# A two-layer streaming trunk on one core: operands turned by one full-height vector instruction per column block, then carried across partitions by 16 on-chip transfers begun by GpSimd

## The chip, the cores and the metric

The kernel runs on one core of one Trainium2 chip. The metric is the device time of an execution in microseconds; the number given for a kernel is the median of its runs. The core has TensorE (PE, with its weight loads PEld), VectorE (DVE), ScalarE (ACT), GpSimd (POOL) and SyncE (SP), which run their own instruction streams and meet at semaphores, and 16 DMA engines that move what the queues of SP, ACT or GpSimd are told to move.

## The reference, cut to what matters

256 tokens of width 2048 go through two layers; every layer adds a mixer, a SwiGLU feed-forward and a gated embedding to the running sum, all with an RMSNorm ahead. Everything is float32.

```
h = x                                        # (1, 256, 2048)
for i in range(2):
    h = h + mixer_i(rmsnorm(h))              # i = 0: top-k attention and gated linear attention
                                             # i = 1: stick-breaking attention, 16 heads of 128
    n = rmsnorm(h);  h = h + (silu(n @ W_gate) * (n @ W_up)) @ W_down        # 5632 wide
    h = h + (p[i] @ W_pe) * sigmoid(rmsnorm(h) @ W_pg)
out = rmsnorm(h)
```

## The kernel before, in words

The sum `h` lies in SBUF with the tokens on the partitions (two halves of 128 tokens, 2048 columns). A product `n @ W` wants the contraction on the partitions, so each stage's operand is `h` turned: 16 chunks of 128 columns, each [128 columns x 256 tokens], times the norm's gain, split in two parts that PE takes in one pass each (`aH` and `aL`). A weight is split likewise into `whi` and `wlo`, and every product is done as three matmuls: hi by hi (L201), hi by lo (L202) and lo by hi (L203).

The weights stream through `unit` (L176): SP loads 1 MB into `raw` (a ring of two), ACT casts it by halves into `whi` (L99), DVE subtracts into `wlo` (L100), rings of four. A half unit is two chunks by 512 output columns: 12 matmuls. A `block` is one block of 512 output columns over the whole contraction, 8 half units where it is 2048 deep.

All other work is filled in between. `later` puts a function into a queue and `tick`, at the end of each half unit, takes one from it; `delay` and `after` say how many half units must pass first; `need` takes what a product can't do without.

What is turned, and how:

- **h, for the norms n1 to n5.** When a column block of h is complete, `finish_cols` (L224) queues two calls of `turn_h` (L135): four PE transposes into PSUM (L141), then ACT writes `aH` (L146) and DVE `aL` (L147) per chunk. n1 leads from the first mixer into the FFN, n2 from the FFN into the embedding, n3 from there into the odd mixer, n4 and n5 as n1 and n2 in the second layer. The first norm, n0, does the same while x arrives.
- **The FFN's hidden blocks.** A block of 512 hidden columns is `sl` (ACT silu, times the up product on DVE, L802). `turn_blocks` (L123) turns it into `hx` by 16 DVE transposes of 32x256 (L128): DVE turns blocks of 32 by 32 and writes them into any quarter of the partitions. `split_hid` (L787) makes `hH` and `hL` of it. There are 11 blocks in each of two layers, in groups of 3, 3, 3 and 2; a group's down product comes a group later.
- **The odd mixer's q and k.** `tok` (L762) is the block scaled by the norm; 16 transposes of the same kind write `qT` or `kT`, 4 blocks each, which the scores on PE read.

`rstd_of` (L113) makes a norm's factor: two DVE instructions, then a power on GpSimd (L119). `ple` (L847) is the embedding; its first four blocks have a contraction of two chunks only, loads of 512 KB. In the last one `keep` (L892) holds the last 256 columns' weights in SBUF, loaded through a buffer of their own.

Of the kernel before, what the change touches and what calls it, by code (L numbers as in the profile page):

```python
# [27 lines left out]
def trunk_kernel(ctx: ExitStack, tc: tile.TileContext, x, p, even_norm, even_w_in, even_w_gk,  # L28
# [36 lines left out]
    # the activation tables and the tensor engine's clock are up when the data comes  # L65
# [7 lines left out]
    # norm gains, one row of 128 per chunk, turned so that a chunk's gains lie along the partitions  # L73
# [49 lines left out]
    def turn_blocks(dst, src, a):  # L123
# [3 lines left out]
        for q in range(4):  # L127
            nc.vector.transpose(dst[32 * a:32 * a + 32, :, :, 32 * q:32 * q + 32],  # L128
                                src.rearrange("p t (m a c) -> p t m a c", a=4, c=32)[32 * q:32 * q + 32, :, :, a, :])
# [5 lines left out]
    def turn_h(dst, norm, c2):  # L135
        """Chunks 2*c2 and 2*c2+1 of h, transposed, times the gain, split."""
# [39 lines left out]
    def unit(ps, stat, k0, cols, first, last, nk=KU, kw0=None, step=KU, pre=None):  # L176
        """nk chunks of the contraction: cols = [(weight, first column, width)]."""
# [28 lines left out]
    def block(stat, cols, nk=KC, key=None, ps=None, k0=0, k1=None, kw=0, pre=None):  # L206
        """Output columns over chunks k0..k1 of the contraction; returns the two PSUM tiles."""
# [43 lines left out]
    with tc.issue_after(got_gains.ins):  # L251
# [4 lines left out]
    # upb[s, c] = 1/16 where s <= c in one chunk of 64; sub[s, c] = 1/16 where s > c there  # L256
    upb = const.tile([P, P], F32, name="upb")
    nc.gpsimd.memset(upb, 0.0625)
    nc.gpsimd.affine_select(upb, upb, pattern=[[1, P]], compare_op=OP.is_ge, fill=0.0, base=0,
                            channel_multiplier=-1)  # L260
    nc.gpsimd.memset(upb[0:64, 64:128], 0.0)
    sub = stage("sub")[:, :P]
    nc.gpsimd.memset(sub, 0.0625)
    nc.gpsimd.affine_select(sub, sub, pattern=[[-1, P]], compare_op=OP.is_gt, fill=0.0, base=0,
                            channel_multiplier=1)
    nc.gpsimd.memset(sub[64:128, 0:64], 0.0)
    subr = const.tile([P, P], F32R, name="subr")
    nc.vector.tensor_copy(subr, sub)
    # keys no later than the query, in one chunk
    upm = upb.bitcast(I32)  # L270
    # strictly earlier keys, keys along the partitions
# [8 lines left out]
    # -1 where the first index is no earlier than the second  # L280
# [10 lines left out]
    def even_mixer(xs, ps0, ep):  # L291
# [3 lines left out]
        oT = new_act()  # L295

# [12 lines left out]
        def tokens(ps, name, w=NB):  # L309
            """The block's last w columns by tokens, scaled by the row's norm."""  # L310
# [672 lines left out]
```

## Time and profile before

| | |
|---|---|
| median of 3 runs | 2442.11 us (2441.62 to 2442.64) |
| span of the profiled execution | 2438.5 us |
| PE busy | 2417.6 us (99%) |
| DVE busy | 1506.6 us (62%) |
| ACT busy | 1154.1 us (47%) |
| GpSimd busy | 19.2 us (1%) |
| share of PE in the chain that ended last | 91% |
| 16 DMA engines, SP's queue | 55.6% |

The span is one execution, taken by the profiler; the median is of other executions, and 3.6 us longer. The chain is the work that ended last, followed back from the end: an engine that has no share in it may be late by something without a change of the time.

### The profile page before, as it was taken

To read this page: it belongs to the slowest core of one execution; us is meant where nothing else is said; L and a number is where in the kernel's file an instruction comes from. 1 tells how busy PE (TensorE), PEld (TensorE's weight loads), DVE (VectorE), ACT (ScalarE), POOL (GpSimd) and SP (SyncE) were. 2 spreads that over 40 slices of the span, in tenths; PEclk is the share of its full clock that TensorE was granted. 3 is DMA by queue.
4 is the path that set the end of the run, shared out by engine and by line. 5 is a ranking of instruction groups with operands and counts; after the bars stand their busy time and mean duration, and the time that the engine had idled before them with its cause. 6 is when DMAs were issued, how large, how long until landed. Compare 5 with 4: busy or idle time off the path is not lost.

```text
span 2438.5 us, 27647 instructions
## 1 busy us (share of the span) xinstructions
PE 2417.6 (99%) x10966; PEld 1996.5 (82%) x10966; DVE 1506.6 (62%) x1907; ACT 1154.1 (47%) x1418; POOL 19.2 (1%) x45
## 2 busy tenths in 40 slices
PE   8999999999999999999999999999999999999998
PEld 7887788888888888888888888888888888888887
DVE  5765555766756665655676666557667556556564
ACT  6644444344434434446546565544444344444463
POOL 0000000000000000000000000000000000000000
PEclk9999999999999999999999999999999999999999
DMA  6454455566556565555554454555655655556563
GB/s 211 147 169 151 144 194 186 189 196 201 189 192 193 186 205 183 198 190 185 178 190 156 161 184 165 180 190 177 203 190 192 205 190 186 196 187 206 182 231 123
DMA packets 231651, 450.01 MB, mean 185 GB/s; under 512 B 9457, under 2 KB 16337, under 8 KB 231394
## 3 DMA queue, kind: packets, MB, share of 16 engines
q1 hardware_dynamic: 231234, 447.07, 55.6%
q8 instruction: 86, 1.41, 0.2%
q10 hardware_dynamic: 288, 1.18, 0.1%
q14 instruction: 43, 0.35, 0.0%
HBM read 446.12 MB, written 2.10 MB: 184 GB/s over the span
## 4 chain that ended last, share of the span: by engine, by line
PE 91%; issue 5%; ACT 2%; DVE 1%; DMA 1%; SPq 0%; POOLq 0%; POOL 0%; DVEq 0%; ACTq 0%
PE mm L202 29%; PE mm L201 29%; PE mm L203 29%; PE at L141 1%; DVE kT L128 1%; DVE wlo L100 0%; DMA raw<-in_odd_w_in_dram 0%; PE at L424 0%; DMA h<-in_x_dram 0%; PE at L742 0%; DVE sp L719 0%; ACT whi L99 0%; ACT sp L716 0%; ACT sp L715 0%; ACT L715 0%
## 5 line engine op out<-in xcount | busy, mean ns | idle before, releaser
L100 DVE TENSOR_TENSOR wlo<-raw,whi 128x1024 fp32r<-128x1024 f32 (+2 forms) x848 | 1020.7, 1213 | 794.1 <-ACT whi L99 790.1
L99 ACT CAST whi<-raw 128x1024 fp32r<-128x1024 f32 (+2 forms) x848 | 874.8, 1042 | 1053.5 <-PE mm L203 668.8
L201 PE MATMUL mm<-whi,aH 128*128 128x512 f32 (+2 forms) x2656 | 1036.9, 390 | 0.7 <-ACT whi L99 0.7
L202 PE MATMUL mm<-wlo,aH 128*128 128x512 f32 (+2 forms) x2656 | 1028.8, 387 | 4.1 <-DVE wlo L100 4.1
L203 PE MATMUL mm<-whi,aL 128*128 128x512 f32 (+2 forms) x2656 | 1028.7, 387 | 0.0
L202 PEld LDWEIGHTS mm<-wlo,aH 128*128 128x128 f32 x2656 | 499.4, 188 | 104.7 <-DVE wlo L100 5.9
L203 PEld LDWEIGHTS mm<-whi,aL 128*128 128x128 f32 x2656 | 499.1, 188 | 103.4 <-issue 1.0
L201 PEld LDWEIGHTS mm<-whi,aH 128*128 128x128 f32 x2656 | 499.2, 188 | 102.9 <-issue 2.8
L201 PE MATMUL mm<-whi,hH 128*128 128x512 f32 x704 | 277.2, 394 | 0.0
L202 PE MATMUL mm<-wlo,hH 128*128 128x512 f32 x704 | 277.0, 393 | 0.0
L203 PE MATMUL mm<-whi,hL 128*128 128x512 f32 x704 | 273.6, 389 | 0.0
L128 DVE STREAM_TRANSPOSE hx<-sl 32x256 f32<-32x256 f32 x352 | 153.6, 436 | 6.1
L201 PEld LDWEIGHTS mm<-whi,hH 128*128 128x128 f32 x704 | 132.2, 188 | 30.0
L203 PEld LDWEIGHTS mm<-whi,hL 128*128 128x128 f32 x704 | 132.2, 188 | 29.7
L202 PEld LDWEIGHTS mm<-wlo,hH 128*128 128x128 f32 x704 | 132.4, 188 | 26.1
L146 ACT ACTIVATE aH<-at,gT 128x256 fp32r<-128x256 f32 x96 | 45.1, 473 | 51.4 <-DVE aL L147 47.5
L789 ACT CAST hH<-hx 128x1024 fp32r<-128x1024 f32 x22 | 23.2, 1054 | 92.6 <-DVE hx L128 92.6
L147 DVE SCALAR_TENSOR_TENSOR aL<-at,gT,aH 128x256 fp32r<-128x256 f32 x96 | 45.8, 480 | 22.0 <-ACT aH L146 21.9
L234 DVE TENSOR_TENSOR h<-mm,h 128x512 f32<-128x512 f32 x80 | 52.4, 682 | 2.7 <-PE mm L203 2.7
L141 PE MATMUL at<-ident,h 128*128 128x128 f32 x192 | 30.5, 283 | 5.0 <-DMA h<-in_x_dram 5.0
L141 PEld LDWEIGHTS at<-ident,h 128*128 128x128 f32 x192 | 24.9, 145 | 11.8 <-DMA h<-in_x_dram 3.0
L128 DVE STREAM_TRANSPOSE qT<-tok 32x256 f32<-32x256 f32 x64 | 27.9, 436 | 6.8 <-ACT tok L762 5.8
(221 smaller groups left out, 806.8 us busy)
## 6 DMA issues: line engine op xcount, KB each, us to landing
raw<-in_ffn_w_gate_dram SPq DMA_DIRECT2D x88, 1024.0 KB, 5.2
raw<-in_ffn_w_up_dram SPq DMA_DIRECT2D x88, 1024.0 KB, 5.2
raw<-in_ffn_w_down_dram SPq DMA_DIRECT2D x88, 1024.0 KB, 5.0
raw<-in_odd_w_in_dram SPq DMA_DIRECT2D x48, 1024.0 KB, 5.2
raw<-in_even_w_in_dram SPq DMA_DIRECT2D x36, 1024.0 KB, 5.0
raw<-in_ple_w_gate_dram SPq DMA_DIRECT2D x28, 1024.0 KB, 5.1
raw<-in_even_w_out_dram SPq DMA_DIRECT2D x16, 1024.0 KB, 5.1
raw<-in_odd_w_out_dram SPq DMA_DIRECT2D x16, 1024.0 KB, 5.0
```

The lines of the kernel that those rows point to most:

```text
L99: nc.scalar.copy(hi, raw)
L100: nc.vector.tensor_tensor(lo, raw, hi.bitcast(F32), OP.subtract)
L128: nc.vector.transpose(dst[32 * a:32 * a + 32, :, :, 32 * q:32 * q + 32], src.rearrange("p t (m a c) -> p t m a c", a=4, c=32)[32 * q:32 * ...
L141: nc.tensor.transpose(ps[:, c, tt, :], h[:, tt, k * P:(k + 1) * P], ident)
L146: nc.scalar.activation(dst[0][:, k, :], src, AF.Copy, scale=g)
L147: nc.vector.scalar_tensor_tensor(dst[1][:, k, :], src, g, dst[0][:, k, :].bitcast(F32), op0=OP.mult, op1=OP.subtract)
L201: nc.tensor.matmul(ps[tt][:, :n], sh, hi[:, c, :n], start=st, stop=False)
L202: nc.tensor.matmul(ps[tt][:, :n], sh, lo[:, c, :n], start=False, stop=False)
L203: nc.tensor.matmul(ps[tt][:, :n], sl, hi[:, c, :n], start=False, stop=en)
L234: nc.vector.tensor_tensor(hs, ps[tt], hs, OP.add)
L789: nc.scalar.copy(d[0], t)
```

## The change

`turn_h` stays for n0 alone. For n1 to n5, for the FFN's blocks and for q and k there is `cross`: one DVE transpose over all 128 partitions and 1024 elements of a block (L130) into `tq`, a single buffer, which turns each 32x32 block in its own 32 partitions; then 16 DMAs from SBUF to SBUF (L135), each of 32 partitions by 1 KB, begun by GpSimd, that carry the quarters of `tq` to the partitions where they belong, in `tx`, a ring of two. There are 20 crossings of h, 22 of hidden blocks and 8 of q and k: 50, with 800 DMAs. What reads the result comes two half units later at the earliest: `gain_h` (ACT L171, DVE L172) for h, `split_hid` (ACT L819, DVE L820), and for q and k one ACT copy (L794) into `qT` or `kT`, whose layout is now by heads.

To find room in SBUF, some things move: constants of the first mixer into its own pool, the scratch of the squares into a shared buffer, `gated` writes in place, and `keep` loads through the stream's `raw` ring. `mixer_out` is cut in two, so that the pool of `tq` and `tx` opens behind the first mixer.

```
+    def cross(src):
+        tq = pools["x"].tile([P, 4, NT, 4, 32], F32, name="tq", bufs=1)
+        nc.vector.transpose(tq.rearrange("p a t m r -> p t m a r"),
+                            src.rearrange("p t (m a c) -> p t m a c", a=4, c=32))
+        x = pools["x"].tile([P, 8, 4, 32], F32, name="tx")
+        for a in range(4):
+            for q in range(4):
+                nc.gpsimd.dma_start(x[32 * a:32 * a + 32, q::4], tq[32 * q:32 * q + 32, a])
+        return x
...
+    def gain_h(dst, norm, x, c2):
+        for k in (2 * c2, 2 * c2 + 1):
+            g = gT[1][:, (norm - 1) * KC + k:(norm - 1) * KC + k + 1]
+            src = crossed(x)[:, k % 4]
+            hi, lo = (flat(d[:, k:k + 1, :])[:, 0] for d in dst)
+            nc.scalar.activation(hi, src, AF.Copy, scale=g)
+            nc.vector.scalar_tensor_tensor(lo, src, g, hi.bitcast(F32), op0=OP.mult, op1=OP.subtract)
...
     def finish_cols(nx, cb):
+        x = {}
+        first = (nx["key"], "x", cb)
+        later(lambda: x.update(x=cross(h[:, :, cb * NB:(cb + 1) * NB])), key=first)
         for c2 in (2 * cb, 2 * cb + 1):
-            later(lambda c2=c2: turn_h(nx["dst"], nx["norm"], c2), key=(nx["key"], c2))
+            later(lambda c2=c2: gain_h(nx["dst"], nx["norm"], x["x"], c2), key=(nx["key"], c2), after=(first, 2))
...
-                for a in range(4):
-                    later(lambda t=t, d=dst, a=a: turn_blocks(d.rearrange("p t (m c) -> p t m c", c=P), t, a))
+                x = {}
+                later(lambda t=t, x=x: x.update(x=cross(t)), key=("x3", g, i))
+                later(lambda d=dst, x=x: nc.scalar.copy(flat(d), crossed(x["x"])), after=(("x3", g, i), 2))
...
-                hx = fp.tile([P, 4, NT * P], F32, name="hx")
-                for a in range(4):
-                    later(lambda d=hx, t=sl, a=a: turn_blocks(d.rearrange("p m (t c) -> p t m c", t=NT), t, a))
-                later(lambda t=hx, n=n, gi=gi: split_hid(hT[gi], t, 4 * n), key=("hT", i, b))
+                x = {}
+                later(lambda t=sl, x=x: x.update(x=cross(t)), key=("xT", i, b))
+                later(lambda x=x, n=n, gi=gi: split_hid(hT[gi], x["x"], 4 * n), key=("hT", i, b),
+                      after=(("xT", i, b), 2))
...
-            sgm = pp.tile([P, NB], F32, name="sgm", bufs=2)[:, :w]
-            nc.scalar.activation(sgm, pg[:, :w], AF.Sigmoid, scale=rs[:, tt:tt + 1])
-            nc.vector.tensor_tensor(sgm, sgm, eb[c0 // NB][tt][:, c0 % NB:c0 % NB + w], OP.mult)
+            nc.scalar.activation(pg[:, :w], pg[:, :w], AF.Sigmoid, scale=rs[:, tt:tt + 1])
+            e = eb[c0 // NB][tt][:, c0 % NB:c0 % NB + w]
+            nc.vector.tensor_tensor(e, pg[:, :w], e, OP.mult)
...
-            raw = pp.tile([P, KU, HB], F32, name="kept", bufs=1)
+            raw = wp.tile([P, KU, NB], F32, name="raw", bufs=2)[:, :, :HB]
```

How the instructions stand on the engines, at three places. First DVE at the first hidden block of the first FFN. Before (`sl` is the block, `hx` it turned, `wlo` the weights' low parts):

```order
L802 SCALAR_TENSOR_TENSOR sl_3289<-mm_3292,rstd_3287,sl_3289 128x512
L802 SCALAR_TENSOR_TENSOR sl_3289<-mm_3293,rstd_3287,sl_3289 128x512
L128 STREAM_TRANSPOSE hx_3432<-sl_3289 32x2x4x32 x8
L100 TENSOR_TENSOR wlo_3496<-raw_3473,whi_3495 128x1024
L128 STREAM_TRANSPOSE hx_3432<-sl_3289 32x2x4x32 x4
L100 TENSOR_TENSOR wlo_3518<-raw_3515,whi_3517 128x1024
L128 STREAM_TRANSPOSE hx_3432<-sl_3289 32x2x4x32 x4
L100 TENSOR_TENSOR wlo_3538<-raw_3515,whi_3537 128x1024
L790 TENSOR_TENSOR hL_3127<-hx_3432,hH_3126 128x1024
```

And now:

```order
L832 SCALAR_TENSOR_TENSOR sl_3328<-mm_3332,rstd_3326,sl_3328 128x512
L130 STREAM_TRANSPOSE tq_3507<-sl_3328 128x8x4x32
L100 TENSOR_TENSOR wlo_3545<-raw_3526,whi_3544 128x1024
L100 TENSOR_TENSOR wlo_3565<-raw_3562,whi_3564 128x1024
L100 TENSOR_TENSOR wlo_3581<-raw_3562,whi_3580 128x1024
L100 TENSOR_TENSOR wlo_3599<-raw_3596,whi_3598 128x1024
L100 TENSOR_TENSOR wlo_3615<-raw_3596,whi_3614 128x1024
L820 TENSOR_TENSOR hL_3157<-tx_3509,hH_3156 128x1024
```

The 16 transposes have become one, and what reads the turned block stands behind five half units' subtractions in place of three; on ACT the cast into `hH` stands behind the same five casts.

The second place is DVE at the end of the first FFN (n2), from the second column block of the down product to the third; `h_73` is h, `at` the PSUM tile of the PE transposes. Before:

```order
L100 TENSOR_TENSOR wlo_8044<-raw_8041,whi_8043 128x1024
L147 SCALAR_TENSOR_TENSOR aL_7730<-at_7965,gT5_95,aH_7729 128x256
L234 TENSOR_TENSOR h_73<-mm_7902,h_73 128x512
L147 SCALAR_TENSOR_TENSOR aL_7730<-at_7965,gT5_95,aH_7729 128x256
L234 TENSOR_TENSOR h_73<-mm_7903,h_73 128x512
L100 TENSOR_TENSOR wlo_8069<-raw_8041,whi_8068 128x1024
```

And now:

```order
L261 TENSOR_TENSOR h_73<-mm_7968,h_73 128x512
L261 TENSOR_TENSOR h_73<-mm_7969,h_73 128x512
L100 TENSOR_TENSOR wlo_8149<-raw_8130,whi_8148 128x1024
L130 STREAM_TRANSPOSE tq_8111<-h_73 128x8x4x32
L172 SCALAR_TENSOR_TENSOR aL_7791<-tx_8010,gT5_95,aH_7790 128x256 x4
L100 TENSOR_TENSOR wlo_8185<-raw_8182,whi_8184 128x1024
L100 TENSOR_TENSOR wlo_8213<-raw_8210,whi_8212 128x1024
```

Every column block's turn into `tq` now stands ahead of the reading of the block before it, and the weights' subtractions stand behind both.

The third place is GpSimd around n3, the norm between the embedding and the odd mixer. Before, from the end of the first mixer on:

```order
L667 TENSOR_TENSOR sg_2464<-sg_2464,gn_1703 128x512 x2
L119 TENSOR_TENSOR rstd_3287<-var_3284,mhalf_96 128x2
L119 TENSOR_TENSOR rstd_8351<-var_8348,mhalf_96 128x2
L119 TENSOR_TENSOR rstd_9046<-var_9043,mhalf_96 128x2
L119 TENSOR_TENSOR rstd_11858<-var_11855,mhalf_96 128x2
```

And now (`x16` is the 16 DMAs of one crossing; `rstd_9171` is n3's):

```order
L135 DMA tx_8849<-tq_8847 32x2x128 x16
L135 DMA tx_9032<-tq_9030 32x2x128 x16
L119 TENSOR_TENSOR rstd_9171<-var_9168,mhalf_96 128x2
L135 DMA tx_9217<-tq_9215 32x2x128 x16
L135 DMA tx_9379<-tq_9377 32x2x128 x16
```

The power for a norm now stands behind the 16 DMAs of the norm's last column block.

## Rows read from the trace of the kernel before

**Rows 1.** The page: engines' busy time, and the chain's shares by engine.
```profile
PE 2417.6 (99%) x10966; PEld 1996.5 (82%) x10966; DVE 1506.6 (62%) x1907; ACT 1154.1 (47%) x1418; POOL 19.2 (1%) x45
...
PE 91%; issue 5%; ACT 2%; DVE 1%; DMA 1%; SPq 0%; POOLq 0%; POOL 0%; DVEq 0%; ACTq 0%
```

**Rows 2.** Costliest groups: line, engine, operation, count | busy us, mean ns | idle before.
```profile
L128 DVE STREAM_TRANSPOSE hx<-sl 32x256 f32<-32x256 f32 x352 | 153.6, 436 | 6.1
...
L146 ACT ACTIVATE aH<-at,gT 128x256 fp32r<-128x256 f32 x96 | 45.1, 473 | 51.4 <-DVE aL L147 47.5
...
L141 PE MATMUL at<-ident,h 128*128 128x128 f32 x192 | 30.5, 283 | 5.0 <-DMA h<-in_x_dram 5.0
```

**Rows 3.** Timeline of PE around a group of transposes: start us, length us, what.
```profile
1085.65 0.40 PE L203 MATMUL mm<-whi,hL 128*128 128x512 f32 x1
1085.89 0.60 PE L141 MATMUL at<-ident,h 128*128 128x128 f32 x4
...
1086.80 0.39 PE L203 MATMUL mm<-whi,hL 128*128 128x512 f32 x1
```

**Rows 4.** Timeline of DVE at the first hidden block.
```profile
431.81 1.22 DVE L100 TENSOR_TENSOR wlo<-raw,whi 128x1024 fp32r<-128x1024 f32 x1 [1.50 <-ACT whi L99]
432.95 1.40 DVE L802 SCALAR_TENSOR_TENSOR sl<-mm,rstd,sl 128x512 f32<-128x512 f32 x2
```

**Rows 5.** Timeline of ACT at the first hidden block.
```profile
430.72 1.05 ACT L99 CAST whi<-raw 128x1024 fp32r<-128x1024 f32 x1 [1.67 <-PE mm L203]
433.44 1.05 ACT L99 CAST whi<-raw 128x1024 fp32r<-128x1024 f32 x1 [1.67 <-PE mm L203]
```

**Rows 6.** Timeline, DVE then ACT, at n1's last column block.
```profile
388.51 1.28 DVE L234 TENSOR_TENSOR h<-mm,h 128x512 f32<-128x512 f32 x2
...
388.96 1.06 ACT L99 CAST whi<-raw 128x1024 fp32r<-128x1024 f32 x1 [1.62 <-PE mm L203]
```

**Rows 7.** Timeline of DVE, two column blocks of n2.
```profile
1065.88 1.28 DVE L234 TENSOR_TENSOR h<-mm,h 128x512 f32<-128x512 f32 x2
...
1076.86 1.28 DVE L234 TENSOR_TENSOR h<-mm,h 128x512 f32<-128x512 f32 x2
```

**Rows 8.** Timeline, ACT then DVE, at n3's last column block.
```profile
1214.27 1.37 ACT L864 ACTIVATE sgm<-mm,rstd 128x512 f32<-128x512 f32 x2 [0.94 <-PE mm L203]
...
1216.28 1.29 DVE L867 TENSOR_TENSOR h<-h,sgm 128x512 f32<-128x512 f32 x2
...
1219.88 0.17 DVE L758 TENSOR_SCALAR rq<-rstd 128x2 f32<-128x2 f32 x1 [0.90 <-POOL rstd L119]
```

**Rows 9.** Timeline of ACT, the first group's k in the odd mixer.
```profile
1259.30 1.31 ACT L762 ACTIVATE tok<-mm,rstd 128x512 f32<-128x512 f32 x2 [0.54 <-PE mm L203]
```

**Rows 10.** Groups of GpSimd: line, operation, shape, count | busy us, mean ns | idle before.
```profile
L667 POOL TENSOR_TENSOR sg<-sg,gn 128x512 f32<-128x512 f32 x4 | 5.1, 1294 | 5.9 <-ACT sg L665 5.9
L119 POOL TENSOR_TENSOR rstd<-var,mhalf 128x2 f32<-128x2 f32 x6 | 4.2, 700 | 2052.0 <-DVE var L117 1327.7 <-ACT pe L856 724.3
L632 POOL TENSOR_TENSOR rso<-rso,mhalf 128x4 f32<-128x4 f32 x2 | 2.0, 1016 | 180.1 <-DVE rso L631 180.1
```

**Rows 11.** The chain at the start: start us, length us, what (SPq issues a load).
```profile
1.71 0.46 SPq L184
```

**Rows 12.** DMA queues (packets, MB, share); loads: count, KB each, median us to landing.
```profile
q1 hardware_dynamic: 231234, 447.07, 55.6%
...
raw<-in_ple_w_gate_dram SPq DMA_DIRECT2D x28, 1024.0 KB, 5.1
...
raw<-in_ple_w_proj_dram SPq DMA_DIRECT2D x8, 512.0 KB, 3.7
...
out_dram<-h SPq DMA_DIRECT2D x8, 256.0 KB, 2.8
...
graw<-in_odd_norm_dram SPq DMA_DIRECT2D x1, 8.0 KB, 1.6
```

More of the change, by code (lines that the diff above doesn't have):

```diff
@@ L107, in square_sum @@
             ss[key] = sm.tile([P, NT, 4], F32, name="ss")
-        scr = sm.tile([P, NB], F32, name="sqs", bufs=1)
+        scr = sm.tile([P, NB], F32, name="sqs", tag="stage", bufs=1)
         nc.scalar.activation(scr, src, AF.Square, accum_out=ss[key][:, tt, cb:cb + 1])
@@ L121, in rstd_of, with crossed, flat @@
         return rstds[key]
[L123 to L129, printed above, removed]
+    pools = {}
+    def cross(src):
[7 more added lines that the diff above has]
+        return x
+    def crossed(x):
+        return x.rearrange("p q m r -> p m q r")
+    def flat(t):
+        return t.rearrange("p m (q r) -> p m q r", q=8)
     def new_act():
@@ L253, in trunk_kernel @@
     done.update((("n0", i), 0) for i in range(KC // 2))
[L257 to L270, printed above, removed]
     diag = const.tile([P, P], F32, name="diag")
@@ L295, in even_mixer @@
         oT = new_act()
+        upb = ep.tile([P, P], F32, name="upb", bufs=1)
+        nc.gpsimd.memset(upb, 0.0625)
+        nc.gpsimd.affine_select(upb, upb, pattern=[[1, P]], compare_op=OP.is_ge, fill=0.0, base=0,
+                                channel_multiplier=-1)
+        nc.gpsimd.memset(upb[0:64, 64:128], 0.0)
+        sub = stage("sub")[:, :P]
+        nc.gpsimd.memset(sub, 0.0625)
+        nc.gpsimd.affine_select(sub, sub, pattern=[[-1, P]], compare_op=OP.is_gt, fill=0.0, base=0,
+                                channel_multiplier=1)
+        nc.gpsimd.memset(sub[64:128, 0:64], 0.0)
+        subr = ep.tile([P, P], F32R, name="subr", bufs=1)
+        nc.vector.tensor_copy(subr, sub)
+        upm = upb.bitcast(I32)
         def t2(name, dt=F32):
@@ L623, in outputs @@
             for a in range(2):
-                scr = sm.tile([P, NB], F32, name="sqs", bufs=1)
+                scr = sm.tile([P, NB], F32, name="sqs", tag="stage", bufs=1)
                 nc.scalar.activation(scr[:, :256], ov[g][:, tt, a * 256:(a + 1) * 256], AF.Square,
@@ L672, in even_mixer, with mixer_out_first, mixer_out @@
         return oT
-    def mixer_out(oT, W, nx):
+    def mixer_out_first(oT, W):
         for i in range(4):
             need(("oT", i))
-        part = {}
-        for cb in range(2):
-            part[cb] = block(oT, [(W, cb * NB, NB)], k1=8)
+        part = [block(oT, [(W, cb * NB, NB)], k1=8) for cb in range(2)]
         for i in range(4, 8):
             need(("oT", i))
+        return part
+    def mixer_out(oT, W, nx, part):
         for cb in range(4):
-            ps = block(oT, [(W, cb * NB, NB)], ps=part.get(cb), k0=8 if cb < 2 else 0)
+            ps = block(oT, [(W, cb * NB, NB)], ps=part[cb] if cb < 2 else None, k0=8 if cb < 2 else 0)
             add_to_h(ps, cb)
@@ L708, in scores @@
                 pz = at_tile()
-                nc.tensor.matmul(pz[:, 0:256], kT[:, 0, js], qT[:, :, js], start=True, stop=False,
+                nc.tensor.matmul(pz[:, 0:256], kT[:, j, 0:P], qT[:, j, :], start=True, stop=False,
                                  skip_group_check=True)
-                nc.tensor.matmul(pz[:, 256:384], kT[:, 1, js], qT[:, 1, js], start=False, stop=False,
+                nc.tensor.matmul(pz[:, 256:384], kT[:, j, P:], qT[:, j, P:], start=False, stop=False,
                                  skip_group_check=True)
@@ L758, in odd_mixer @@
                     nc.vector.tensor_scalar(rq, rs, float(128 ** -0.5), None, op0=OP.mult)
-                dst = op.tile([P, NT, NB], F32, name="qT" if i == 0 else "kT")
+                dst = op.tile([P, 4, NT * P], F32, name="qT" if i == 0 else "kT")
                 t = op.tile([P, NT, NB], F32, name="tok")
@@ L785, in ffn, with split_hid @@
         hT = {}
-        def split_hid(dst, t, k0):
-            d = [dst[n][:, k0:k0 + 4, :] for n in range(2)]
-            nc.scalar.copy(d[0], t)
-            nc.vector.tensor_tensor(d[1], t, d[0].bitcast(F32), OP.subtract)
+        def split_hid(dst, x, k0):
+            hi, lo = (flat(dst[n][:, k0:k0 + 4, :]) for n in range(2))
+            nc.scalar.copy(hi, crossed(x))
+            nc.vector.tensor_tensor(lo, crossed(x), hi.bitcast(F32), OP.subtract)
         def gate_up(gi):
@@ L885, in squared @@
             c0, w = parts[n]
-            scr = sm.tile([P, NB], F32, name="sqs", bufs=1)
+            scr = sm.tile([P, NB], F32, name="sqs", tag="stage", bufs=1)
             nc.scalar.activation(scr[:, :w], h[:, tt, c0:c0 + w], AF.Square, scale=float(D ** -0.5),
@@ L939, in trunk_kernel @@
         nx = start_norm("n1", 1)
-        mixer_out(oT, even_w_out[0], nx)
+        part = mixer_out_first(oT, even_w_out[0])
+    pools["x"] = ctx.enter_context(tc.tile_pool(name="xp", bufs=2))
+    mixer_out(oT, even_w_out[0], nx, part)
     with tc.tile_pool(name="fp0", bufs=2) as fp:
@@ L950, in trunk_kernel @@
         nx = start_norm("n4", 4)
-        mixer_out(oT, odd_w_out[0], nx)
+        mixer_out(oT, odd_w_out[0], nx, mixer_out_first(oT, odd_w_out[0]))
     with tc.tile_pool(name="fp1", bufs=2) as fp:
```

2 lines of the change are left out of this document (1 added, 1 removed).

## The prediction

> **What bounds the kernel now.** I read the page's busy shares and its chain first, then the rows of the places that the change touches. TensorE is busy for 2417.6 of 2438.5 us and holds 91% of the chain [rows 1]: time leaves only with PE instructions, and comes only where PE is made to wait. PE works at the pace of the weights' half units: two casts of `whi` start 2.72 us apart [rows 5], which is one half unit of 12 matmuls. The ring of four `whi` lets the cast run three half units ahead; with a cast of 1.05 and a subtraction of 1.22 us [rows 4, 5] the work on ACT and DVE can be late by about 3 x 2.72 - 1.05 - 1.22 = 5.9 us before PE stands. GpSimd does almost nothing [rows 1], and has no DMA.
>
> **What the change removes.** The 40 groups of four transposes on PE (5 norms x 8). Between the starts of the two L203 around such a group there are 1086.80 - 1085.65 = 1.15 us where three matmuls without it take 0.68 (a quarter of 2.72), so a group costs 0.47 us [rows 3] and all 40 cost **-18.8 us**, all on the path. On DVE 480 transposes of 0.436 us go [rows 2], 209 us, and 50 full-height ones come. Such a one has four times the elements; it lies between 1.22, the 128x1024 subtraction [rows 4], and 4 x 0.436 = 1.74; I take 1.24, since its engine time should go by elements as that of the subtraction does, and it makes 62 us. DVE is off the path, so its 147 us give nothing by themselves. All waits of PE together are at most 2438.5 - 2417.6 = 20.9 us [rows 1], most of it at the start; I count no gain from there.
>
> **What it adds: 800 transfers on GpSimd's queue.** This is the price that decides, and the trace of before has no such issue. Below it is bounded by the issues of SP, 0.46 us each [rows 11], above by what GpSimd takes for one small instruction, 0.70 us for a 128x2 power, 1.02 for a 128x4 one, 1.29 for 128x512 [rows 10]. Below zero it can't go: no issue stood there. I take 0.70: the nearest row on the same engine. The last of the 16 then lands some time after its issue: 8 KB took 1.6 us, 256 KB 2.8 [rows 12]; for 32 KB I take 2.0. So one **chain** lasts 16 x 0.70 + 2.0 = 13.2 us (9.4 at 0.46; 18.3 at 1.02). The bytes point the same way. Queue q1 moves 231,234 packets in 55.6% of 16 engines' time [rows 12]: 93.8 ns for one. A crossing has 16 x 64 = 1024 pieces of 512 B; at that price they take 6.0 us of all 16 engines, and beside weights that want 55.6% they need 6.0 / 0.444 = 13.6 us, even if the issue is cheap. Smaller pieces may be faster, so this is an upper bound for the transport.
>
> First what a row shows of GpSimd's own cost: 0.70 us for the smallest power instruction [rows 10]. The Trainium skill (DMA: Bandwidth & Descriptors, Specifications and SWDGE vs HWDGE vs iDMA) says that a transfer begun by GpSimd has its descriptors computed in software, with about 1 us to the first byte, where SP's queue has hardware for it. If that were the time of each issue, a chain would be 18 us and the sum that of the second rival below. No row here shows it.
>
> **Who waits for a chain, place by place** (rooms are estimates from the rows named and the order of the instructions).
>
> 1. FFN, 22 blocks. DVE is done with `sl` at 432.95 + 1.40 = 434.35 [rows 4], turned at 435.6. The cast of `hH` stands behind five casts of weights. Those start at 433.44 and then every 2.72 [rows 5], the sixth nominally at 447.04; with the cover of 5.9 it may start at 452.9, and `hH` (1.05 us) before it at 451.9. Room 16.3: a chain of 13.2 is hidden. **0.** (What covers it is the ring, and each us beyond costs 22 us.)
> 2. Odd mixer, kT, 4 groups. The scores stand on PE five half units, 13.6 us, behind the block of k. `tok` takes 1.3 us [rows 9], the turn 1.24, the copy from tx 1.05: room 13.6 - 3.6 = 10.0, less some 0.2 of handoffs, 9.8. **4 x 3.4 = +13.6.**
> 3. The last column block of the even layer's embedding into the odd mixer (n3). The block ends at 1214.2, when ACT's sigmoid starts [rows 8]; chunk 12 is wanted six half units later, 1230.5. h is done at 1217.57 [rows 8], one subtraction of 1.22 comes first, turned at 1220.0; the first `aH` and `aL` take 0.47 each [rows 2]. Room 9.6: **+3.6.** The three blocks ahead of it have their four `aH` (1.9 us) behind five casts: the next cast's half unit starts 21.8 us behind the block's end, so they must begin 21.8 - 1.05 - 1.22 - 1.9 = 17.6 behind it; turned after 5.8, the room is 11.8: **3 x 1.4 = +4.2.**
> 4. Mixer into FFN (n1, n4). The block ends with the half unit that frees the cast at 388.96; h is done at 388.51 + 1.28 [rows 6], turned at 391.0, chunk 12 wanted at 388.9 + 16.3 = 405.2: room 13.2, **0**. It is as tight as a place can be.
> 5. FFN into the embedding (n2, n5). The last group's column blocks come every 1076.86 - 1065.88 = 10.98 us [rows 7], but `tq` is a single buffer: the next turn waits on DVE until the 16 transfers have landed, 1.24 + 13.2 = 14.4 us after the last. Queued behind that turn are the weights' subtractions, so PE stands. Three gaps of 3.5 are 10.5 us at each of two places; the cover could take 5.9 of it. I take it whole, because the embedding's first loads are of half size, 3.7 us to land [rows 12], and leave the ring little lead: **+21** (9 with the cover).
>
> **The kept weights.** The four loads of 512 KB move from a buffer of their own into the stream's two `raw` slots. While one sits there, the next 1 MB load (5.1 us [rows 12]) has no second slot; each can cost 0 to 3.5 us. I take 2: **+8** (0 to 14). The writes in place in PSUM and the moved constants change nothing on PE: 0.
>
> Also queued on GpSimd: the power for a norm's `rstd` now stands behind 16 issues. At n3, DVE waited 0.90 us for it [rows 8]; in the changed order it comes some 11 us later, before the block that uses it ends 21.8 us on. 0.
>
> **The sum:** -18.8 + 13.6 + 3.6 + 4.2 + 21 + 8 = +31.6. The profiled execution has a span of 2438.5, 3.6 us under the median of 2442.1; I put the sum on the median: **2474 us**, with 2455 to 2492 as this case's own range (issue of 0.60 to 0.75 and the cover at place 5).
>
> **The rivals.**
>
> *The chain is short* (issue as SP's, 0.46, chain 9.4). Then kT, n3 and `tq` (1.24 + 9.4 = 10.6 against 10.98) all fit; -18.8 + 8 = -11: **2431**, 2423 with the kept loads free. For it: SP's rows are of the same kind of instruction. Against: another engine, 16 in a row, and the packets' 13.6. From about 0.54 us per issue on the sum turns positive.
>
> *The chain is longer than the FFN's room* (issue 1.02, chain 18.3): 22 x 2.0 = 44 at the FFN, kT 4 x 8.5 = 34, n2 and n5 6 x 8.6 = 51.5, n3 8.7 + 3 x 6.5 = 28, n1 and n4 2 x 5.1 and about 17 for their earlier blocks, with -11: +174, **2616**. It decides against the kernel from 16.3 us per chain, 0.89 per issue. For it: GpSimd's rows of 1.02 and 1.29. Against: those compute on more elements, an issue on none.
>
> *GpSimd's issue only runs while DVE is idle.* DVE is busy 62% of the span [rows 1]; an issue of 0.46 that proceeds in the other 38% takes 1.2 us, a chain 21.2: by the same places some +300, **2743**. Against: the power's 128x2 instances kept to a mean of 0.70 beside a busy DVE [rows 10].
>
> The Trainium skill (SBUF — State Buffer, A bandwidth-pool intuition that's wrong, and the warning above it) describes such a lock: GpSimd can't write descriptors while DVE runs a two-port copy, 620 ns alone becoming some 3100 beside one. Its case is a DVE copy, while DVE here mostly does two-input subtractions; no row shows what those do to an issue.
>
> **How the numbers follow.** Forecast 0.38 (2474). Short chain 0.29 (2431). Issue near the turning point, 0.52 to 0.56, within 0.2%: 0.06. Long chain 0.19 (2616). Lock 0.08 (2743). A measurement here can tell about 0.2%, 4.9 us, from no change. Faster is the short chain, 0.30 with rounding; slower 0.64. The cases of both signs hold much, so the range reaches from the short chain with free kept loads to past the long one: 2420 to 2690, leaving out the lock and the far end of the long chain. Predicted is the likeliest, 2474.
>
> **What would show it.** On GpSimd's queue, rows of L135 with their spacing: 0.70 confirms, under 0.5 or over 0.9 gives the rivals. PE's L141 rows of n1 to n5 must be gone (32 of 192 stay). PE idle times ended by ACT or DVE must stand at n2, n5, kT and n3 and not in the FFN; if the FFN's casts of `whi` show waits behind `hH<-tx` with PE idle, the chain is over 16.3. DVE's L130 rows must show a wait for the DMA at n2 and n5 only. The prediction is wrong if the issue price is, since each 0.1 us is 1.6 us at up to 50 places.

## The result, and the profile after

The changed kernel takes **2515.05 us** (median of 4 runs, 2512.55 to 2516.8) against 2442.38 of the kernel before on the same chip: the ratio is **1.0299**, 95% interval 1.0284 to 1.0313. That is 73 us slower; 32 were forecast. The side was right and the time lies inside the range, but the sum holds only 32 of the 73 us, and the rest of this document is about which of its terms were short.

The page after, in parts. The engines (busy us, share, instructions), to be set against [rows 1]:

```profile
PE 2432.1 (97%) x10806; PEld 1996.4 (79%) x10806; DVE 1352.1 (54%) x1477; ACT 1161.3 (46%) x1426; POOL 442.4 (18%) x845
```

Two of its DMA queues (packets, MB, the time of the packets as a share of 16 engines' span):

```profile
q1 hardware_dynamic: 231234, 447.07, 54.3%
q0 software_dynamic: 25600, 26.27, 3.8%
```

Its group of GpSimd's issues (busy us, mean ns of one, idle time before them), and its row of the transfers (KB each, median us from issue to landing):

```profile
L135 POOL DMA_DIRECT2D tx<-tq x800 | 421.6, 535 | 1674.0 <-issue 1013.6
...
tx<-tq POOLq DMA_DIRECT2D x800, 32.0 KB, 4.0
```

PE has 160 instructions fewer, as the change says, and yet more busy time (2432.1 against 2417.6): its matmuls became slower in places. GpSimd's issue takes 0.535 us, not the 0.70 that I took; a transfer lands 4.0 us after its issue in the middle, not 2.0. The transfers are 25,600 packets of about 1 KB, half as many as I had counted, and take 3.8% of the engines' time.

What PE waited for, in the whole execution (us in all, times, longest):

```profile
PE at L738 <- ACT kT L794: 18.5, 4, 7.4
PE mm L225 <- ACT pe L886: 14.0, 2, 10.3
PE mm L226 <- DVE wlo L100: 13.9, 20, 1.4
PE mm L225 <- ACT whi L99: 11.4, 8, 2.2
PE mm L225 <- ACT aH L171: 8.2, 2, 5.5
```

Before, the only entries of weight were the arrival of x (5.0) and `wlo` (4.1). To place the loss I set the starts of the same instructions of both traces side by side: the end of each stretch, and what it adds to the lateness. The last column is the same for the first experiment below, in which nothing is transferred.

| stretch, up to | before, us | after, us | adds | adds without transfers |
|---|---|---|---|---|
| first hidden block of FFN 0 (start, n1) | 432.95 | 437.12 | +4.2 | -4.0 |
| last group of FFN 0 begins its down product | 1065.88 | 1071.32 | +1.3 | 0.0 |
| first gated block of embedding 0 (n2) | 1149.38 | 1162.07 | +7.2 | -3.6 |
| tok of the first k (embedding 0, n3) | 1259.30 | 1284.79 | +12.8 | -3.8 |
| first sum of the odd mixer's output (q, k) | 1546.80 | 1590.50 | +18.2 | -5.5 |
| first hidden block of FFN 1 (n4) | 1648.57 | 1694.62 | +2.4 | -3.4 |
| last group of FFN 1 begins its down product | 2281.49 | 2331.32 | +3.8 | -0.4 |
| first gated block of embedding 1 (n5) | 2367.71 | 2427.79 | +10.3 | -5.9 |
| end (kept weights) | 2438.52 | 2515.08 | +16.5 | +16.5 |
| all | | | +76.6 | -10.3 |

The difference of the two last columns is what the chains of transfers cost, with all that hangs on them: 8.2, 1.3, 10.9, 16.6, 23.7, 5.8, 4.2, 16.2 and 0, in all 86.9 us. These are single executions; by the medians the change costs 72.7 us, not 76.6.

**A chain.** GpSimd at the first hidden block (start us, length us, count, idle before):

```profile
440.38 4.78 POOL L135 DMA_DIRECT2D tx<-tq  x9 [32.52 <-issue]
445.82 0.53 POOL L135 DMA_DIRECT2D tx<-tq  x1 [0.66 <-DMA tx<-tq]
447.43 3.16 POOL L135 DMA_DIRECT2D tx<-tq  x6 [1.07 <-DMA tx<-tq]
```

Nine issues run through, then one waits for an earlier transfer to land: each of the 16 waits for the one eight before it (the two that stand here start 0.3 us behind that landing). The first starts 0.6 us behind the turn, the 16 take 10.2 us, and the last lands 2.1 us behind the end of its issue: 12.9 from turned to landed. Over all 50 crossings the middle is 13.3 us, as forecast, from 11.6 to 17.8; ten of them are over 15.

### The profile page after: what moved, and what is told of

It is laid out like the page before. It is cut to its first block, busy times and chain, and to the rows that moved or that the text cites. A ratio compares the mean times of both kernels' runs of the same rounds, so it can differ in the third digit from the quotient of the medians.

```text
span 2515.1 us, 28154 instructions
## 1 busy us (share of the span) xinstructions
PE 2432.1 (97%) x10806; PEld 1996.4 (79%) x10806; DVE 1352.1 (54%) x1477; ACT 1161.3 (46%) x1426; POOL 442.4 (18%) x845
## 3 DMA queue, kind: packets, MB, share of 16 engines
q0 software_dynamic: 25600, 26.27, 3.8%
## 5 line engine op out<-in xcount | busy, mean ns | idle before, releaser
L135 POOL DMA_DIRECT2D tx<-tq x800 | 421.6, 535 | 1674.0 <-issue 1013.6
L226 PEld LDWEIGHTS mm<-wlo,aH 128*128 128x128 f32 x2656 | 503.4, 190 | 119.9 <-DVE wlo L100 18.8
L820 DVE TENSOR_TENSOR hL<-tx,hH 128x1024 fp32r<-128x1024 f32 x22 | 27.0, 1225 | 86.9 <-ACT hH L819 86.9
L171 ACT ACTIVATE aH<-tx,gT 128x256 fp32r<-128x256 f32 x80 | 34.6, 498 | 78.2 <-DMA tx<-tq 78.2
L819 ACT CAST hH<-tx 128x1024 fp32r<-128x1024 f32 x22 | 23.1, 1050 | 90.7 <-DMA tx<-tq 90.7
L172 DVE SCALAR_TENSOR_TENSOR aL<-tx,gT,aH 128x256 fp32r<-128x256 f32 x80 | 33.7, 478 | 52.6 <-ACT aH L171 52.6
L829 ACT ACTIVATE sl<-mm,rstd 128x512 f32<-128x512 f32 x44 | 29.6, 686 | 17.8 <-PE mm L227 17.8
L130 DVE STREAM_TRANSPOSE tq<-h 128x1024 f32<-128x1024 f32 x20 | 24.8, 1242 | 18.9 <-DMA tx<-tq 18.6
```

Of the source, the lines that this page charges most:

```text
L130: nc.vector.transpose(tq.rearrange("p a t m r -> p t m a r"), src.rearrange("p t (m a c) -> p t m a c", a=4, c=32))
L135: nc.gpsimd.dma_start(x[32 * a:32 * a + 32, q::4], tq[32 * q:32 * q + 32, a])
L171: nc.scalar.activation(hi, src, AF.Copy, scale=g)
L172: nc.vector.scalar_tensor_tensor(lo, src, g, hi.bitcast(F32), op0=OP.mult, op1=OP.subtract)
L226: nc.tensor.matmul(ps[tt][:, :n], sh, lo[:, c, :n], start=False, stop=False)
L820: nc.vector.tensor_tensor(lo, crossed(x), hi.bitcast(F32), OP.subtract)
```

## The experiments

Times before are those of the same session, 2440.8 to 2441.7 us; the changed kernel, by its ratio, stands at 2514 beside them.

**1. No transfers.** In `cross`:

```
-        tq = pools["x"].tile([P, 4, NT, 4, 32], F32, name="tq", bufs=1)
+        tq = pools["x"].tile([P, 4, NT, 4, 32], F32, name="tq")
...
-        x = pools["x"].tile([P, 8, 4, 32], F32, name="tx")
-        for a in range(4):
-            for q in range(4):
-                nc.gpsimd.dma_start(...)
-        return x
+        return tq.rearrange("p a t m r -> p (a t) m r")
```

> The 16 transfers of each crossing are left out and the readers take the turned block itself, so the quarters stay in the wrong partitions; all else is as in the changed kernel. Theory (the chains of transfers, 13.3 us in the middle and up to 17.8, are what PE waits for): all stalls but those of the kept weights go, the removed PE transposes stay removed: 2442 - 18.8 + 16 = 2439 us, 2432 to 2446, and the granted clock back at 0.995 or more. Rival (the later readers, the single turn or the moved buffers cost it): above 2480. Third view (the kept loads' 16 us were a follow-up of the stalls ahead of them): 2423.

Measured: 2430.79 us, ratio 0.996 (0.9945 to 0.9974). PE's largest waits (us in all, times, longest):

```profile
PE mm L221 <- ACT whi L99: 5.9, 4, 2.5
PE at L152 <- DMA h<-in_x_dram: 5.0, 2, 2.8
PE mm L222 <- DVE wlo L100: 2.7, 3, 1.4
```

The transfers cost the 83 us between this and 2514; the turn in one instruction, the later readers and the moved buffers do not. Here `tq` is read directly and is a ring of two, so this run does not tell the transfers from the waits for the single `tq` that they cause. It is also lower than I expected. Up to the kept weights it is 26.7 us ahead of the kernel before, not 18.8: the odd mixer gains 5.5 us, where 3.9 us of PE's waits for `wlo` and `whi` have become 0.2, and n5 2 us more than its transposes. The end gives back 16.5 of it.

**2. The kept weights out of the stream's ring.**

```
-            raw = wp.tile([P, KU, NB], F32, name="raw", bufs=2)[:, :, :HB]
+            raw = pools["x"].tile([P, KU, HB], F32, name="kept", tag="tx")
```

> The kept weights' four loads go through the buffers of tx, which are idle by then, in place of the stream's two raw slots. Theory (a kept load takes a slot away from the stream, 16 us between the embedding's second and fourth block): 2515 - 16 = 2499 us. Rival (the loss there comes from the late operand of n5 and not from the slots): 2513 to 2516. My forecast had 8 us for this.

Measured: 2506.03 us, 1.0266 (1.0251 to 1.0281), 8 us less. In its trace the last stretch adds 3.1 us in place of 16.5. In the changed kernel SP's queue stands there like this, by the timeline (start us, length us; L208 is a 1 MB load, L924 a kept one):

```profile
2432.01 0.37 SPq L208 DMA_DIRECT2D raw<-in_ple_w_gate_dram  x1
2433.75 0.37 SPq L924 DMA_DIRECT2D raw<-in_ple_w_gate_dram  x1
2440.61 0.37 SPq L208 DMA_DIRECT2D raw<-in_ple_w_gate_dram  x1
```

and ACT's casts of the same loads (in brackets the idle time before, and what ended it):

```profile
2437.14 1.99 ACT L99 CAST whi<-raw 128x1024 fp32r<-128x1024 f32 x2 [5.65 <-DMA raw<-in_ple_w_gate_dram]
2439.04 1.04 ACT L99 CAST wh<-raw 128x1024 fp32r<-128x1024 f32 x1
2445.88 2.00 ACT L99 CAST whi<-raw 128x1024 fp32r<-128x1024 f32 x2 [5.80 <-DMA raw<-in_ple_w_gate_dram]
```

The next 1 MB is issued 8.6 us after the last, when the kept load has left its slot, and its casts start 8.7 us behind those of the load before, where PE's two half units take 5.4 (twice 2.72 [rows 5]). Some of the gain is lost again elsewhere (the stretch of n5 came out 4 us worse in that execution), so 8 to 13 us is what this part is worth.

**3. Only the FFN's blocks carried**, in the kernel before: `split_hid` and the hidden blocks of the change, with the scratch of the squares in the shared buffer as there, the rest unchanged.

```
-  later(lambda d=hx, t=sl, a=a: turn_blocks(...))
+  later(lambda t=sl, x=x: x.update(x=cross(t)), key=("xT", i, b))
```

> The kernel before, with only the FFN's 22 hidden blocks carried by GpSimd; h, q and k are turned as before, the kept weights have their own buffer. Theory (room of 16.3 us hides a chain of 13.3; only the few chains above 16.3 reach PE): 2442 to 2448 us, no PE transposes being removed. Rival (22 places each lose a little): 2455 or more. Second rival (DVE freed of 352 transposes helps): below 2438.

Measured: 2447.32 us, 1.0027 (1.0017 to 1.0036). The 22 crossings of the FFN cost little: the trace puts 2.7 us on the two FFNs. The other 3.7 lie behind the last matmul of the kernel, and I have no cause for them. That the FFN's room hides a middling chain is confirmed.

**4. Scores later.**

```
-  later(... nc.scalar.copy(flat(d), crossed(x["x"])), after=(("x3", g, i), 2))
+  later(... nc.scalar.copy(flat(d), crossed(x["x"])), after=(("x3", g, i), 4))
...
-  later(... scores(q, k, pair), key=("z", g, pair["heads"]))
+  later(... scores(q, k, pair), key=("z", g, pair["heads"]), after=(("x3", g, 1), 6))
```

> The changed kernel with the copies of qT and kT two half units and the scores about three half units later. Theory (PE waited 18.5 us at the scores for the transfers of kT): the room grows from 9.8 to about 18 us, PE does not wait there: 2515 - 18 = 2497 us. Rival (the wait only moves, to the copy on ACT with the casts queued behind it, or to the shares and the next group's q): 2508 or more.

Measured: 2503.87 us, 1.0258 (1.0241 to 1.0275), 10 us less. PE's wait at the scores:

```profile
PE at L738 <- ACT kT L794: 1.8, 1, 1.8
```

18.5 us have become 1.8, and the odd mixer adds 1.6 us in place of 18.2. The rest came back upstream: n1 and n2 cost 5 us more in this execution than in that of the changed kernel, by longer chains. So the place is settled; the whole time moves by less, since chains differ between executions.

**5. Half of the transfers.**

```
-            for q in range(4):
+            for q in range(2):
                 nc.gpsimd.dma_start(x[32 * a:32 * a + 32, q::4], tq[32 * q:32 * q + 32, a])
+        nc.gpsimd.memset(x[:, 2:4], 0.0)
+        nc.gpsimd.memset(x[:, 6:8], 0.0)
```

> Only 8 of the 16 transfers of each crossing are begun; the other half of tx is set to zero by two small GpSimd instructions, so half of each turned block is left out. Theory (PE waits for the length of a chain; 8 issues of 0.53 us need no wait for an earlier landing and end after about 4.8 + 3 to 5 us of landing, 8 to 10 us): all rooms of 9.6 us and more hold, the kernel is near the one without transfers, 2431 to 2440 us, of which 16 are the kept weights. Rival (a fixed price for each crossing, whatever its length, such as the first landing or the order of the readers): half of the loss or more stays, 2470 or above.

Measured: 2489.52 us, 1.0195 (1.0181 to 1.0209), far above what I expected. The chains are 8.0 us in the middle, as expected, with no wait for an earlier landing. But the readers moved: the order in which instructions are put on ACT is worked out when the kernel is built, and with 8 transfers the reader of a column block stands behind three casts, no longer five. ACT's timeline at n4's first column block, turned at 1561.2:

```profile
1561.80 1.06 ACT L99 CAST whi<-raw 128x1024 fp32r<-128x1024 f32 x1 [0.28 <-PE mm L229]
1564.52 1.06 ACT L99 CAST whi<-raw 128x1024 fp32r<-128x1024 f32 x1 [1.66 <-PE mm L229]
1573.33 1.72 ACT L173 ACTIVATE aH<-tx,gT 128x256 fp32r<-128x256 f32 x4 [7.75 <-DMA tx<-tq]
```

and GpSimd's:

```profile
1561.45 0.54 POOL L135 DMA_DIRECT2D tx<-tq  x1 [57.50 <-DVE tq L130]
1564.85 3.70 POOL L135 DMA_DIRECT2D tx<-tq  x7 [2.86 <-issue]
```

ACT waits 7.75 us at the reader, with the next casts behind it; 2.86 of them are a pause in GpSimd's chain (last section), but at n1's third block, whose eight issues run through, ACT waits longer still:

```profile
382.96 1.71 ACT L173 ACTIVATE aH<-tx,gT 128x256 fp32r<-128x256 f32 x4 [8.98 <-DMA tx<-tq]
```

So the whole time, which is in the rival's range, does not tell a price per crossing from a price by length, as I had meant: the room shrank with the chain, by two half units, 5.4 us. At two places the trace does tell: the odd mixer adds -6.5 us in place of 18.2 (PE's wait for `kT` is 1.2) and n3 2.9 in place of 12.8, so there the length was the price; n1, n2 and n4 add more than in the changed kernel, 5.4, 10.8 and 8.8, and n5 9.5. That the order is part of the cost is read from these places; no run changes the order alone.

**6. Begun by SyncE** (`nc.sync.dma_start` in place of `nc.gpsimd.dma_start`).

> The same 16 transfers, begun by SyncE on the queue that also loads the weights. If the price is GpSimd's own, the software that makes its descriptors, a chain falls to 16 x 0.46 + 2 = 9.4 us and the time to 2440 to 2460. Theory (an issue costs about as much there, 0.46 against 0.53 us, and the landing of 1.2 to 6 us comes from the weights in flight): chains of 11 to 15 us stay, and the weights' loads now queue behind the issues: 2500 to 2560.

Measured: 2748.41 us, 1.1266 (1.1245 to 1.1288). The row of the transfers:

```profile
tx<-tq SPq DMA_DIRECT2D x800, 32.0 KB, 1.9
```

PE's largest wait (us in all, times, longest):

```profile
PE mm L225 <- ACT whi L99: 175.8, 53, 7.2
```

An issue takes 0.595 us there and a chain 11.7 in the middle, so GpSimd's 0.535 is no dearer than SP's queue. The landing is 1.9 where it was 4.0: SP issues the weights and these transfers in one order, and no new weight load starts while a chain is being issued. That is also why it is so slow: the loads of the weights stand behind each chain, and PE waits 176 us for `whi`. They stand behind the turn as well, for which SP waits in the same order (us in all, times, longest):

```profile
SPq L135 <- DVE tq L130: 195.1, 44, 7.3
```

I had expected that direction, not the size. Of the changed kernel's own transfers, those issued while a weight load was in flight (611 of 800, by the loads whose landing the trace tells, 386 of 440) landed 3.6 us behind the end of their issue in the middle, the others 2.7; so the weights go with a part of the landing.

**7. n2 and n5 carried by halves** (blocks 2 and 4 turned by PE).

```
+        if nx["norm"] in (2, 5) and cb % 2:
+            for c2 in (2 * cb, 2 * cb + 1):
+                later(lambda c2=c2: turn_h(nx["dst"], nx["norm"], c2), key=(nx["key"], c2))
+            return
```

> At n2 and n5 only the first and third column block are carried by GpSimd, 21.9 us apart; the second and fourth are turned by PE as before. Theory (crossings of 14 us every 11 us pile up at the single tq and stall DVE and PE by some 23 us at the two places): those 23 us go, 8 groups of PE transposes come back at 3.8: about 2514 - 23 + 3.8 = 2494 us, and DVE's waits of tq for landings, 18.6 us in four pieces, vanish. Rival (PE stands there because the embedding's first loads are of half size): 2508 or more.

Measured: 2500.04 us, 1.024 (1.0226 to 1.0254). The total fits, the place does not. DVE's waits for landings before `tq`, in the changed kernel

```profile
DVE tq L130 <- DMA tx<-tq: 18.6, 4, 6.6
```

are gone, but n5 still adds 10.3 us, as in the changed kernel, and n2 5.0 in place of 7.2, with four groups of PE's transposes (1.9 us) back in each. Of the 20 us between the two profiled executions the largest part, 7.5, is in the odd mixer: its last wait for `kT` is 2.1 us in place of 7.4, because the pause of GpSimd's queue that had hit that chain falls elsewhere when there are 32 issues fewer ahead of it (last section). That part of the match is luck. ACT at n5:

```profile
2370.60 0.91 ACT L171 ACTIVATE aH<-tx,gT 128x256 fp32r<-128x256 f32 x2 [11.15 <-DMA tx<-tq]
...
2373.43 1.04 ACT L890 COPY pe<-mm 128x512 f32<-128x512 f32 x2
```

ACT stands 11.15 us at the reader `aH<-tx`, and the copies that empty the embedding's PSUM tiles are queued behind it; PE has no tile to write into. This chain took 17.6 us, with a pause of GpSimd in it:

```profile
2363.40 1.59 POOL L135 DMA_DIRECT2D tx<-tq  x3 [2.87 <-issue]
```

So my theory that the single `tq` is what stops PE falls: PE stands there without any wait for it, by way of ACT's reader. That `tq` had no share in the changed kernel is not shown: there the turn of this place's third block stood 5.22 us for it, and ACT's reader behind that chain.

```profile
2373.01 1.25 DVE L130 STREAM_TRANSPOSE tq<-h 128x1024 f32<-128x1024 f32 x1 [5.22 <-DMA tx<-tq]
```

**8. Three together**: the edits of 2, 4 and 7 in one kernel.

> Scores later, kept weights in the buffers of tx, and n2 and n5 carried by halves, all three in one kernel. Theory (each takes away a wait of its own place): the three gains, about 10, 8 to 10 and 15 us, add up: 2514 - 34 = 2480 us, 2475 to 2487, with PE's waits at the scores, at the first blocks of the embedding and for tq gone, and those of n1, n3 and n4 left. Rival (one late stage feeds the next, so that the waits overlap and move): above 2490.

Measured: 2471.95 us, 1.0133 (1.0116 to 1.015), 42 us less than the changed kernel, 34 expected and 32 by the three runs alone, so it lies below the range that I gave. PE's largest waits left:

```profile
PE mm L225 <- ACT pe L891: 11.5, 2, 8.0
PE mm L225 <- ACT aH L171: 10.7, 3, 7.4
```

The gains at least add; the first row is the one of experiment 7.

**9. n2 and n5 by PE alone**, in the kernel of 8.

```
-        if nx["norm"] in (2, 5) and cb % 2:
+        if nx["norm"] in (2, 5):
```

> As the kernel with the three changes together, and nothing of n2 and n5 is carried by GpSimd: PE turns all four column blocks there. In the kernels with the first and third block carried, PE still lost 4.2 us from the end of the first FFN to the first gated block and 11.3 us at the second, with ACT waiting 11 us at the reader of a crossed block and the embedding's copies out of PSUM queued behind that reader. Theory (that reader on ACT is what stops PE there, not the single tq, whose waits were already gone): both terms fall to between -1 and 1 us, and the time from 2472 to about 2457, 2452 to 2461. Rival (the half-size loads of the embedding, or the moved gated, cost it whatever turns the operand): at least 8 of the 15 us stay, 2464 or more.

Measured: 2465.13 us (2459.84 to 2470.89), 1.0107 (1.009 to 1.0124). The wait of PE for `pe` is gone from the list; the two stretches add 0.0 and -2.6 us in place of 4.2 and 11.3. The profiled execution, 2459.84, is within what I expected; the median is 4 us above it and within the rival's range, although nothing is left of the 15 us at the two places. What came back in the profiled execution is 4.9 us at n4 (6.4 in place of 1.5), where one of GpSimd's pauses now falls into the last block's chain:

```profile
1630.30 1.06 POOL L135 DMA_DIRECT2D tx<-tq  x2 [2.87 <-issue]
```

Kernels with crossings of h differ by 4 to 12 us between runs, the first experiment by 3, the kernel before by up to 4.

**10. Where there is room.** Six crossings only, with the kept weights as in 2; FFN, q and k are turned as before.

```
+    BY_X = {1: (0, 2), 2: (0,), 3: (), 4: (0, 2), 5: (0,)}
...
+        if cb not in BY_X[nx["norm"]]:
+            for c2 in (2 * cb, 2 * cb + 1):
+                later(lambda c2=c2: turn_h(nx["dst"], nx["norm"], c2), key=(nx["key"], c2))
+            return
```

> A version of both: only the column blocks that have room are carried by GpSimd (n1 and n4: first and third; n2 and n5: first), in all 6 of 50; the FFN's blocks, q, k and the rest of h are turned as before, the kept weights go through a buffer beside the stream. 12 groups of PE transposes are saved, 5.6 us. Theory: 2436 to 2440 against 2441 of before, 0.1 to 0.2% faster. Rival (any crossing disturbs its surroundings by more than the 0.94 us that two groups cost): 2441 to 2450.

Measured: 2443.26 us, 1.0004 (0.9995 to 1.0012): no difference that can be told, and the rival's range. The 5.6 us of transposes saved are lost again: in the profiled execution, the slowest of the 11, most at n1, which adds 4.0 us and whose two crossings took 14.6 and 16.1 us, then 2.7 in the last stretch and 1.4 at n4. No version that I found carries operands in this way and beats the kernel before.

## Why the prediction was wrong, point by point

**The removal, -18.8: too small.** It measured -26.7 (the first experiment). The 0.47 us per group was right, 4.0 at n1 against 3.8; what I left out is PE's waits in the odd mixer, which gains 5.5 us. I had called nearly all of PE's idle time a matter of the start, but the list of waits of the kernel before has (us in all, times, longest)

```profile
PE mm L202 <- DVE wlo L100: 4.1, 5, 0.8
```

and four of these five, 0.84 us each, are in the odd mixer, behind k's transposes in the chain that ended last; they are gone without the 16 transposes of a block. The rest of the 5.5 and n5's 2 us have no cause on record.

**The length of a chain: right by luck, by errors that cancel.** 13.2 forecast, 13.3 in the middle. Issue 0.535 (0.70 taken, the nearest of GpSimd's own rows; SP's 0.46 [rows 11] was nearer), landing 4.0 (2.0 taken), and waits for the transfer eight before, which I had not priced. Of transport, 1 KB packets took some 60 ns, 1.9 us of all engines for a crossing, not 6.0 (and 6.0 / 0.444 is 13.5, not 13.6).

**One length for all: the step that failed, with the cover.** I set one number, 13.2, against rooms of 9.6 to 16.3. Ten chains of 50 were over 15. So n1, n4 and the FFN, forecast at 0, cost 8.2, 5.8 and 5.5 us; with 8.8 more than forecast at n3, 10.1 at `kT` and 6.1 at n2 and n5 that is the 44.5 us by which the chains were short. And ACT's lead, the cover of 5.9 us in the room of the FFN, is not always there. ACT at n1's third column block, turned at 371.9:

```profile
373.35 2.00 ACT L99 CAST whi<-raw 128x1024 fp32r<-128x1024 f32 x2 [1.85 <-DMA raw<-in_even_w_out_dram]
380.08 2.01 ACT L99 CAST whi<-raw 128x1024 fp32r<-128x1024 f32 x2 [4.73 <-DMA raw<-in_even_w_out_dram]
387.21 1.70 ACT L171 ACTIVATE aH<-tx,gT 128x256 fp32r<-128x256 f32 x4 [5.13 <-DMA tx<-tq]
388.82 3.87 ACT L99 CAST whi<-raw 128x1024 fp32r<-128x1024 f32 x4
```

The casts come in pairs, when 1 MB has landed, after ACT has stood 4.73 us for it, where before the casts wait for PE instead (1.62 us at this norm [rows 6]), that is, ACT is ahead; then ACT waits 5.13 at the reader, and four casts are done back to back. PE's last product before is at 387.61, its next at 389.90. My room for such a block was 15.5 us by the order; the chain was 15.2, and PE stood.

**The clock: not in the sum at all.** PE's timeline at the wait of n5:

```profile
2382.15 0.40 PE L227 MATMUL mm<-whi,pL 128*128 128x512 f32 x1
2392.89 0.79 PE L225 MATMUL mm<-whi,pH 128*128 128x512 f32 x1 [10.35 <-ACT pe L886]
2393.49 0.63 PE L226 MATMUL mm<-wlo,pH 128*128 128x512 f32 x1
2393.91 0.63 PE L227 MATMUL mm<-whi,pL 128*128 128x512 f32 x1
...
2399.20 0.39 PE L225 MATMUL mm<-whi,pH 128*128 128x512 f32 x1
2399.43 0.39 PE L226 MATMUL mm<-wlo,pH 128*128 128x512 f32 x1
```

Windows of 4 us around it (from and to, length, busy us of PE, PEld, DVE, ACT, POOL; granted clock; DMA share; GB/s):

```profile
2384.00:2388.00 4.00, 0.00 (x0) 0.00 (x0) 0.00 (x0) 0.00 (x0) 0.90 (x2) 0.90 0.95 335
2388.00:2392.00 4.00, 0.00 (x0) 0.00 (x0) 1.92 (x3) 1.94 (x6) 0.10 (x1) 0.50 0.41 140
2392.00:2396.00 4.00, 3.10 (x7) 2.48 (x8) 1.84 (x6) 3.24 (x6) 4.00 (x8) 0.50 0.18 49
2396.00:2400.00 4.00, 4.00 (x16) 3.21 (x15) 1.72 (x2) 2.86 (x4) 4.00 (x9) 0.82 0.69 178
```

PE stands 10.35 us; the granted clock falls to 0.50, the level of 1.2 GHz, and stays there after PE has work again: its matmuls start 0.42 us apart (2393.49 to 2393.91) where the full clock has 0.23 (2399.20 to 2399.43). Counted over the trace, 103 products of the weights start 0.36 to 0.48 us behind the last, 12 in the kernel before and 29 without transfers: by estimate some 74 x 0.2 = 15 of the 87 us, about a sixth. The mean granted clock is 0.986 against 0.999, and 0.997 without transfers. So a wait costs more than its length. This was not tested by itself (a wait of PE with the clock held up); it is read from the spacing.

**Place by place:** kT forecast 13.6, PE's wait 18.5 and the whole stretch 23.7 with the clock and the lost gain: mechanism right, shown by experiment 4, size short. n3 and its blocks 7.8, measured 16.6: right mechanism by the wait for `aH<-tx` (5.5 us at n3's last block, at 1254.3; the other piece of the 8.2 is at n4, at 1665.9, which I had at 0), size short. n2 and n5 21, measured 27.1: the size near, the mechanism at best half right. DVE's waits for `tq` came, 18.6 us, but what PE waits for is ACT's reader with the copies `pe` behind it, and it does so without any wait for `tq` (experiments 7 and 9). I had named what is queued behind DVE's wait and not what is queued behind ACT's.

**The kept weights:** 8 forecast, 16.5 measured by the trace, also without transfers: 4.1 for each of the four, above the bound "0 to 3.5 each". Experiment 2 took 13.4 of it away by its trace and 8 by the whole time.

**The rivals.** The short chain, 0.29, did not happen: its issue price nearly did (0.535), the landing did not. The lock between DVE and GpSimd did not show: of 800 issues the middle is 0.533 us and the longest 0.74, beside a DVE that is busy half of the time. The Trainium skill's case of such a lock (SBUF — State Buffer, A bandwidth-pool intuition that's wrong) is a copy on DVE that holds the port; with what DVE does here the trace shows no such stretching. The Trainium skill's 1 us to the first byte for GpSimd's transfers (DMA: Bandwidth & Descriptors, Specifications) lies near the shortest landing, 1.2 us behind the end of the issue, and above the issue's own 0.533.

The arithmetic of the sum, then: -26.7 in place of -18.8, chains 86.9 in place of 42.4, kept weights 16.5 in place of 8; 76.7 by the traces in place of 31.6.

## What to carry to other kernels

A transfer that replaces work on a saturated engine must be priced by its longest instances and by the reader's place in the queue of the engine that waits for it: ask what is queued behind that reader, and who needs it. Price a wait of TensorE as its length plus the matmuls that follow at the lower clock. And when a buffer is taken from a stream's ring for something else, count the loads that then have only one slot.

## What the runs showed that I had not expected

GpSimd's queue has pauses of 2.8 to 2.9 us in the middle of a chain, in which it waits for nothing that the profile names. This is the 39th crossing of 50:

```profile
1828.44 2.24 POOL L135 DMA_DIRECT2D tx<-tq  x4 [33.37 <-issue]
1833.55 4.21 POOL L135 DMA_DIRECT2D tx<-tq  x8 [2.87 <-issue]
```

They go by the number of transfers begun. In the changed kernel they stand ahead of the 250th, 371st, 492nd, 613th and 734th issue, 121 apart, and the 129th, the first of its chain, starts 2.9 us later than the first issues around it. In every other kernel here in which GpSimd begins them they stand at the same counts, as far as its issues reach (2.3 to 3.1 us), whatever crossing that is: in experiment 5, with 8 issues a crossing and two more instructions of GpSimd, the 250th is in another crossing, as shown there. Where SP begins them (experiment 6) there are none. In a window around the one above (1827 to 1836) the queue for instructions (q14) moves a packet; in that of experiment 5 no queue for instructions does, so a loading of GpSimd's program is not what they have in common. What is, stays open.

These pauses are in the five longest chains, 17.0 to 17.8 us. A change that takes crossings away moves them to other places, so that a place can gain or lose what it was not meant to: the odd mixer in experiment 7, n4 in experiment 9. And the issue of a transfer by SP, 0.595 us in a row of 16, is longer than by GpSimd, 0.535.
